# A three-product float32 matmul whose 512-column product is issued as two of 256 columns, in one block of a decoder trunk

## The chip, the cores and the metric

The kernel runs on one core of a Trainium2 chip. The metric is the device time of one execution in microseconds (us), lower is better. Engines are named as in the profile: PE is TensorE's matmul and PEld its weight load, DVE is VectorE, ACT is ScalarE, POOL is GpSimd, SP is the engine that issues most of the transfers.

## The reference, cut to what matters

Four residual layers over one stream of 256 tokens by 1024 features. Each layer is a token mixer and a squared-ReLU MLP, each behind an RMS norm. The second layer (index 1) has a block-sparse attention as its mixer, whose blocks are as long as the sequence, so that it is plain causal attention here.

```python
for i in range(DEPTH):                       # DEPTH = 4, mixers 0, 1, 2, 0
    a = rms_norm(h, attn_norm_g[i])
    ...
        y = moba_attention(a, moba_w_in[slot], moba_w_out[slot], cos, sin)
    ...
    h = h + y
    h = h + sqrelu_mlp(rms_norm(h, mlp_norm_g[i]), mlp_w_up[i], mlp_w_down[i])
```

`moba_attention` ends with `o @ w_out`, a product of 256x1024 with 1024x1024: the out projection. `sqrelu_mlp` is `(relu(h @ w_up) ** 2) @ w_down` with 4096 features between. All of it is float32.

## The kernel before, in words

**Numbers in two parts.** A float32 value is kept as a high part of type `float32r`, which TensorE multiplies at one pass, and a low part, the rest. A product is then three products: high by high, high by low and low by high. Weights come in 185 pieces of 128x2048 floats (1 MB each). `fetch` (L173) issues their transfers on SP. `stage` (L185) splits a piece in two halves of 1024 columns: ACT copies the high part (`whi`, L194), DVE subtracts it for the low part (`wlo`, L195). `take` (L204) hands out the next piece, with pieces staged two ahead (`LOOK`) and fetched five ahead (`FAR`). `whi` and `wlo` have three buffers each and `raw` four, so a piece is split only when TensorE has done with the piece three before it, and its transfer waits for the split of the piece four before it.

**A step.** Activations lie transposed, features on the partitions, as tiles of 128 x (2, 256): high parts of the 256 tokens, then low parts. `block_step` (L803) issues a step of one block of 128 outputs and one block of 128 inputs. One product takes the high weights with all 512 columns, into both halves of a PSUM bank; a second takes the low weights with the 256 high columns, into the bank's first half. Line L134 issues every matmul, so the profile tells them apart by their tiles alone. `joined` (L809) adds the halves: ACT copies the second (`cross`, L812), DVE adds (L813).

**The second layer's out projection** (`out_proj`, L848). Outputs 0 to 3 (128 features each) are accumulated in four banks `p_d`. Outputs 4 to 7 follow one after the other in banks `p_e`: for each of two weight pieces (`j`) and each of two blocks (`b`) eight steps over the inputs (`k`), whose activations are the tiles `oo`. After each block `into` (L815) adds the bank to the residual stream `hT` (DVE, L825), makes the normed stream's two parts `hg` (ACT L351, DVE L352) and its squares (ACT L356, DVE L361).

**The up projection** (`up_proj`, L866). Sixteen groups of two blocks, one piece of weights each, in banks `p_up` (four of them, so that a group reuses the banks of the group two before it). The first group goes over the inputs in the outer loop, so that it starts before the last `hg` is there, and the scheduler puts products of the second group between. Each group's banks are joined into `relu`, squared to `u` (DVE L890) and split to `uu` (ACT L892, DVE L893). In the second group's time the row of the norm is summed on POOL and its reciprocal taken on DVE (L1035). The down projection follows (`p_down`).

**What sets the order.** Each engine runs its instructions in the order of the program. A scheduler of the language makes that order from the dependencies, its own estimate of times and the pools' buffers; pairs listed by hand in `TURNS` set some orders of the mixers and the out projections, none of them in the block that the change touches.

Of the kernel before, what the change touches and what calls it, by code (L numbers as in the profile page):

```python
# [19 lines left out]
P = 128  # L20
# [131 lines left out]
def trunk(ctx: ExitStack, tc: tile.TileContext, xT, gains, lams, swa_row, fng, weights, out):  # L152
    nc = tc.nc
    V, A, G, T = nc.vector, nc.scalar, nc.gpsimd, Numbered(nc.tensor)
# [6 lines left out]
    def bank(tag, name):  # L161
        return ps.tile([P, 512], F32, tag=tag, name=name, bufs=4)
# [41 lines left out]
    def take():  # L204
        i = used[0]
        used[0] += 1
        while len(fetched) < min(weights.shape[0], i + FAR + 1):
            fetch()
        while len(staged) < min(weights.shape[0], i + LOOK + 1):
            stage()  # L210
        return staged[i]

    def r3(n):
        return lambda t: t.rearrange("p (a b) -> p a b", a=n)
# [586 lines left out]


    def block_step(p, hi, lo, x, start, stop, which="hl"):  # L803
        if "h" in which:
            T.matmul(r3(2)(p), hi, x, start=start, stop=False, skip_group_check=True)
        if "l" in which:
            T.matmul(p[:, :S], lo, x[:, 0], start=False, stop=stop, skip_group_check=True)
# [7 lines left out]
    def into(n, d, p, row, whole=False):  # L815

        j, b = d // 2, d % 2
        h = hT[j][:, S * b:S * b + S]
        y = p
        if not whole:  # L820
            y = sb.tile([P, S], F32, tag="y", name="y")
            joined(y, p)
        if row is not None:
            V.tensor_tensor(y, y, row, op=OP.mult)
        V.tensor_tensor(h, y, h, op=OP.add)  # L825
        norm_part(n, d)
        if b:
            norm_sum(n, j)
# [19 lines left out]
    def out_proj(parts, n, rest):  # L848

        banks = [bank("acc", f"p_d{j}") for j in range(4)]  # L850
        two = [[r3(4)(x) for x in take()] for _ in range(2)]
        order = [(k, d) for k in range(6) for d in range(4)] + [(k, d) for d in range(4) for k in (6, 7)]
        for k, d in order:
            hi, lo = (x[:, k % 4, P * d:P * d + P] for x in two[k // 4])
            block_step(banks[d], hi, lo, parts[k], k == 0, k == 7)
            if k == 7:
                into(n, d, banks[d], None)
        for j in range(2):
            hi, lo = (r3(8)(x) for x in take())
            for b in range(2):  # L860
                p = bank("acc", f"p_e{b}")
                for k in range(8):
                    block_step(p, hi[:, k, P * b:P * b + P], lo[:, k, P * b:P * b + P], parts[k], k == 0, k == 7)
                into(n, 4 + 2 * j + b, p, None)

    def up_proj(n, then):  # L866

        us = []
        for g in range(16):
            hi, lo = (r3(8)(x) for x in take())  # L870
            ps_up = [bank("wk", "p_up") for _ in range(2)]
            order = [(b, k) for b in range(2) for k in range(8)]
            if g == 0:
                order.sort(key=lambda x: x[1])

            def up(b, k, which):
                w = slice(P * b, P * b + P)
                block_step(ps_up[b], hi[:, k, w], lo[:, k, w], n.both[k // 2][:, k % 2], k == 0, k == 7, which)

            steps = [(x, "hl") for x in order]  # L880
            if g == 0:

                steps[7:10] = [(order[7 + x], w) for x, w in ((0, "h"), (1, "h"), (0, "l"), (2, "h"), (1, "l"), (2, "l"))]
            for (b, k), which in steps:
                up(b, k, which)
            t = sb.tile([P, 512], F32, tag="relu", name="relu")
            for b in range(2):
                joined(t[:, S * b:S * b + S], ps_up[b])
            u = sb.tile([P, 512], F32, tag="u", name="u")
            V.scalar_tensor_tensor(u, t, 0.0, t, op0=OP.max, op1=OP.mult)  # L890
            both = room(g, [P, 2, 2, S], "uu", F32R)
            A.activation(both[:, :, 0], r3(2)(u), AF.Copy)  # L892
            V.tensor_tensor(both[:, :, 1], r3(2)(u), f(both[:, :, 0]), op=OP.subtract)  # L893
            us += [both[:, b] for b in range(2)]
            then(g)
# [128 lines left out]
    for i in range(DEPTH):  # L1024
        T.layer = i
        parts, rest = mixer_layer(i, n)
# [98 lines left out]
```

## Time and profile before

| | us |
|---|---|
| three runs: lowest, median, highest | 1127.28, 1128.29, 1130.89 |
| the profiled execution | 1127.19 |
| its span, first to last instruction | 1125.4 |
| mean clock that TensorE was granted | 0.998 |

The costliest groups on TensorE, from the page: line, engine, operation, output and inputs, size, count, busy us and mean ns of one, idle time before them.

```profile
L134 PE MATMUL p_up<-hg,whi 128*128 128x512 f32 x1024 | 355.2, 394 | 0.0
L134 PE MATMUL p_up<-hg,wlo 128*128 128x256 f32 x1024 | 283.0, 277 | 0.0
L134 PE MATMUL p_down<-uu,whi 128*128 128x512 f32 x768 | 266.4, 394 | 0.0
```

The matmuls are pipelined: the durations of neighbours overlap, so that the mean of one is longer than the distance between two starts. Where a view gives the idle time before an instruction, what follows the arrow is the engine, tile and line that ended it. In a timeline, rows of one group that stand together are merged, with their count behind the x.

### The profile page before, as it was taken

The page shows a single profiled execution, that of the slowest core. Times are in us where ns is not written, and L with a number is a line of the kernel's source. Part 1 is how long each engine was busy: PE and PEld are TensorE (multiplying, and loading weights), DVE is VectorE, ACT ScalarE, POOL GpSimd, SP SyncE. Part 2 cuts the span into 40 slices and gives each one's busy share as a digit, 9 for nine tenths or more (in the row PEclk, how much of TensorE's full clock was granted, in tenths as well). Part 3 has the DMA queues.
Part 4 walks back from the last instruction along what each step waited for, and adds up shares of the span by engine and source line. Part 5 has one row for each costly group of instructions (what it writes and reads, how often), then busy time and mean ns, then how long its engine had stood idle before and what let it go on. Part 6 is the DMA issues. An engine that isn't in the chain of part 4 may idle for free.

```text
span 1125.4 us, 17122 instructions
## 1 busy us (share of the span) xinstructions
PE 1118.3 (99%) x6478; PEld 974.8 (87%) x6478; DVE 840.3 (75%) x1609; ACT 652.3 (58%) x1183; POOL 136.6 (12%) x273
## 2 busy tenths in 40 slices
PE   9999999999999999999999999999999999999997
PEld 7889888888888888888899998888888899888886
DVE  8888977656687798766569888765568788878453
ACT  7776666544476666554446765554446676555342
POOL 2250000000145200000000000000012410002800
PEclk9999999999999999999999999999999999999999
DMA  9533555555544446555563346555554444654551
GB/s 331 203 132 132 191 208 195 191 188 188 178 159 150 149 152 223 189 187 188 187 211 113 113 151 225 187 187 188 187 187 150 154 146 153 221 188 169 187 187 38
DMA packets 30466, 198.67 MB, mean 177 GB/s; under 512 B 3504, under 2 KB 5040, under 8 KB 7216
## 3 DMA queue, kind: packets, MB, share of 16 engines
q1 hardware_dynamic: 30096, 197.09, 50.6%
q8 instruction: 51, 0.84, 0.3%
q10 hardware_dynamic: 288, 0.49, 0.1%
q14 instruction: 31, 0.25, 0.1%
HBM read 196.52 MB, written 1.05 MB: 176 GB/s over the span
## 4 chain that ended last, share of the span: by engine, by line
PE 97%; DVE 1%; issue 1%; DMA 0%; SPq 0%; ACT 0%; POOLq 0%; POOL 0%; DVEq 0%
PE p_up L134 32%; PE p_down L134 24%; PE p_in L134 19%; PE p_last L134 7%; PE p_d L134 7%; PE p_s L134 3%; PE p_av L134 2%; PE p_qk L137 1%; PE p_t L137 1%; PE p_e L134 1%; DMA raw<-in_weights 0%; DVE wlo L195 0%; PE p_o L137 0%; DVE hg L352 0%; DVE acc L361 0%
## 5 line engine op out<-in xcount | busy, mean ns | idle before, releaser
L195 DVE TENSOR_TENSOR wlo<-raw,whi 128x1024 fp32r<-128x1024 f32 (+1 forms) x374 | 451.1, 1219 | 180.6 <-ACT whi L194 180.1
L194 ACT ACTIVATE whi<-raw 128x1024 fp32r<-128x1024 f32 (+1 forms) x374 | 383.8, 1045 | 200.3 <-issue 112.9
L134 PE MATMUL p_up<-hg,whi 128*128 128x512 f32 x1024 | 355.2, 394 | 0.0
L134 PE MATMUL p_up<-hg,wlo 128*128 128x256 f32 x1024 | 283.0, 277 | 0.0
L134 PE MATMUL p_down<-uu,whi 128*128 128x512 f32 x768 | 266.4, 394 | 0.0
L134 PEld LDWEIGHTS p_up<-hg,whi 128*128 128x128 f32 x1024 | 191.8, 188 | 44.0
L134 PE MATMUL p_down<-uu,wlo 128*128 128x256 f32 x768 | 212.7, 277 | 0.0
L134 PE MATMUL p_in<-whi,hg 128*128 128x512 f32 (+1 forms) x736 | 211.3, 370 | 0.0
L134 PEld LDWEIGHTS p_up<-hg,wlo 128*128 128x128 f32 x1024 | 192.3, 188 | 0.4
L134 PEld LDWEIGHTS p_down<-uu,whi 128*128 128x128 f32 x768 | 144.0, 188 | 33.4
L134 PEld LDWEIGHTS p_in<-whi,hg 128*128 128x128 f32 x736 | 132.3, 189 | 24.0 <-DVE hg L352 1.2
L134 PEld LDWEIGHTS p_down<-uu,wlo 128*128 128x128 f32 x768 | 144.2, 188 | 0.0
L134 PE MATMUL p_in<-wlo,hg 128*128 128x512 f32 (+1 forms) x368 | 130.1, 368 | 0.1
L892 ACT ACTIVATE uu<-u 128x512 fp32r<-128x512 f32 x64 | 40.4, 632 | 80.2 <-DVE u L890 80.2
L134 PE MATMUL p_d<-oo,whi 128*128 128x256 f32 (+1 forms) x416 | 85.2, 296 | 0.0
L134 PE MATMUL p_last<-whi,uu 128*128 128x512 f32 (+1 forms) x264 | 79.4, 383 | 0.0
L134 PEld LDWEIGHTS p_in<-wlo,hg 128*128 128x128 f32 x368 | 68.8, 189 | 11.5 <-DVE wlo L195 0.5
L812 ACT ACTIVATE cross<-p_up 128x256 f32<-128x256 f32 x128 | 47.9, 374 | 35.5 <-PE p_up L134 34.1
L134 PEld LDWEIGHTS p_d<-oo,whi 128*128 128x128 f32 x416 | 66.3, 191 | 1.9 <-issue 0.2
L351 ACT ACTIVATE hg<-hT,gn 128x256 fp32r<-128x256 f32 x64 | 31.4, 503 | 60.5 <-DVE hT L825 60.5
L476 ACT ACTIVATE e<-ns,nm 128x128 f32<-128x128 f32 (+1 forms) x128 | 56.8, 446 | 13.8 <-DVE nm L473 13.8
L518 POOL MEMSET kpadh<- 64x512 f32 x8 | 4.2, 521 | 494.3 <-PE p_down L134 494.1
(179 smaller groups left out, 1235.1 us busy)
## 6 DMA issues: line engine op xcount, KB each, us to landing
raw<-in_weights SPq DMA_DIRECT2D x181, 1024.0 KB, 4.9
raw<-in_weights SPq DMA_DIRECT2D x8, 256.0 KB, 4.8
raw<-in_weights SPq DMA_DIRECT2D x4, 512.0 KB, 7.0
hT<-in_xT SPq DMA_DIRECT2D x8, 128.0 KB, 4.7
bias<-in_swa_row SPq DMA_DIRECT2D x1, 512.0 KB, 4.2
grow<-in_fng SPq DMA_DIRECT2D x1, 512.0 KB, 3.8
lv<-in_lams SPq DMA_DIRECT2D x1, 256.0 KB, 6.6
out<-given ACTq DMA_DIRECT2D x1, 256.0 KB, 2.7
```

What stands on the lines that cost most here:

```text
L134: return self.keep(out.tensor.name.rstrip("_0123456789"), self.engine.matmul(out, *args, **kw))
L137: return self.keep(out.tensor.name.rstrip("_0123456789"), self.engine.transpose(out, *args, **kw))
L194: high = A.activation(hi[:, s], raw[:, s], AF.Copy)
L195: low = V.tensor_tensor(lo[:, s], raw[:, s], f(hi[:, s]), op=OP.subtract)
L351: A.activation(both[:, 0], h, AF.Copy, scale=g)
L476: A.activation(e[:, s], ns[:, s], AF.Exp, bias=nm[:, t:t + 1], scale=-1.0, accum_out=l[:, t:t + 1])
L518: G.memset(f(kpad[x][HD * (1 - h):HD * (1 - h) + HD, :, h, :]), 0.0)
L812: A.activation(cross, p[:, S:], AF.Copy)
L892: A.activation(both[:, :, 0], r3(2)(u), AF.Copy)
```

## The change

In the last block of the second layer's out projection (`j` = 1, `b` = 1, outputs 896 to 1023) the product of the high weights with 512 columns is issued as two products of 256 columns: with the activations' high parts into the bank's first half, then with their low parts into its second half. The product with the low weights stays. This is done for each of the eight `k`. Only the first product of the block starts the bank. The arithmetic is the same.

```diff
     def block_step(p, hi, lo, x, start, stop, which="hl"):
+        if "H" in which:
+
+            for h in range(2):
+                T.matmul(r3(2)(p)[:, h], hi, x[:, h], start=start and h == 0, stop=False, skip_group_check=True)
         if "h" in which:
             T.matmul(r3(2)(p), hi, x, start=start, stop=False, skip_group_check=True)
         if "l" in which:
...
                 for k in range(8):
-                    block_step(p, hi[:, k, P * b:P * b + P], lo[:, k, P * b:P * b + P], parts[k], k == 0, k == 7)
+                    block_step(p, hi[:, k, P * b:P * b + P], lo[:, k, P * b:P * b + P], parts[k], k == 0, k == 7,
+                               "Hl" if j and b else "hl")
                 into(n, 4 + 2 * j + b, p, None)
```

The orders of the two built programs, compared engine by engine (buffer numbers aside): TensorE has 6362 products instead of 6354, eight of 512 columns being sixteen of 256. Besides, one product moves: ahead of the first group's last four products (those with the last tile `hg3`'s second block) stood five products of the second group, now four, and the fifth follows behind the four.

```text
before: p_up (group 2) x5, p_up (group 1)<-hg3 x4, p_up (group 2) ...
after:  p_up (group 2) x4, p_up (group 1)<-hg3 x4, p_up (group 2) ...
```

In the following two groups ACT and DVE take a few instructions in another order (the splits of pieces 68 and 69 against `cross`, `relu`, `u` and `uu` of the second and third groups), and SP's transfer of piece 73 waits for one more semaphore. From the fourth group on, and ahead of the changed block, the orders are the same.

## The prediction

> **What bounds the kernel now.** I read the page first: its busy line, its slices of the granted clock, and the shares of the chain that ended last.
>
> ```profile
> span 1125.4 us, 17122 instructions
> PE 1118.3 (99%) x6478; PEld 974.8 (87%) x6478; DVE 840.3 (75%) x1609; ACT 652.3 (58%) x1183; POOL 136.6 (12%) x273
> ...
> PEclk9999999999999999999999999999999999999999
> ...
> PE 97%; DVE 1%; issue 1%; DMA 0%; SPq 0%; ACT 0%; POOLq 0%; POOL 0%; DVEq 0%
> ```
>
> TensorE is busy 99% of the span, and 97% of the chain is its matmuls. The kernel is a stream of products at an undiminished clock, so a change on TensorE counts in full unless a wait lies behind it, and a change elsewhere counts only if TensorE comes to stand. Next I read the chain of waits in order of time, at the place of the change:
>
> ```profile
> 386.50 5.88 PE p_d L134 x33
> 392.37 11.09 PE p_e L134 x64
> 403.47 88.83 PE p_up L134 x512
> 492.30 88.75 PE p_down L134 x512
> ```
>
> The 64 products of `p_e` give the features 512 to 1023 of the second layer's out projection. The last 16 of them are changed (8 with the high weights, 8 with the low). The up projection follows with no gap. Its 512 products and those of the down projection have the same shapes, 256 pairs of 512 and 256 columns, yet take 88.83 and 88.75 us: some 0.08 us are lost in the up projection. That loss becomes a term below.
>
> **The products themselves.** The timeline of TensorE shows the pace. The columns are start, duration, engine, line, operation; durations overlap, so the pace is the distance of the starts.
>
> ```profile
> 400.53 0.39 PE L134 MATMUL p_e<-oo,whi 128*128 128x512 f32 x1
> ...
> 402.96 0.39 PE L134 MATMUL p_e<-oo,whi 128*128 128x512 f32 x1
> 403.19 0.28 PE L134 MATMUL p_e<-oo,wlo 128*128 128x256 f32 x1
> ```
>
> These are the first and the last high product of the changed block. Seven steps in 402.96 - 400.53 = 2.43 us are 0.347 us for a step of 512 + 256 columns, and the 512 take 403.19 - 402.96 = 0.23 of them. After the change a step is three products of 256 columns, the first two with the same weights. The trace has just that pattern, in the third layer's out projection: high weights twice, low weights once, each of 256 columns.
>
> ```profile
> 644.22 0.28 PE L134 MATMUL p_d<-oo,wlo 128*128 128x256 f32 x1
> ...
> 651.42 0.28 PE L134 MATMUL p_d<-oo,wlo 128*128 128x256 f32 x1
> ```
>
> Twenty steps lie between these two rows, so a step takes 7.20 / 20 = 0.360 us. The change removes 8 products of 512 columns and adds 16 of 256 with 8 more weight loads; it costs 8 x (0.360 - 0.347) = **0.10 us**, directly on the path. The bounds: if a product of 256 columns takes half of one of 512, 8 x (2 x 0.115 - 0.23) = 0; if every added weight load were exposed, what the rival below gives. I take 0.10, from the row with the same shapes, weights and order. A window over that stretch shows why the halves do not get cheaper, and that the clock holds:
>
> ```profile
> 644.20:651.40 7.20, 7.20 (x62) 7.20 (x61) 0.38 (x1) 0.00 (x0) 1.00 0.33 108
> ```
>
> TensorE's weight loads (the fourth column) fill 7.20 of 7.20 us there at clock 1.00: with 256 columns the loads stand back to back, and the pace is theirs. The Trainium skill, "TensorE: Matmul & The Clock Gate", section "Back-to-back issue gap", gives the isolated gap as the columns over 2.4 plus 2.5 ns; two halves would cost 2.5 ns more than the whole, by which I estimate 0.02 us for the eight steps. The trace disagrees in size (0.10), not in sign, and the measurement stands.
>
> **What the instruction order adds.** I compared the two built programs engine by engine. Besides the split there is one move on TensorE. The up projection's first group must end with the last block of the normed stream (`hg3`), which is made from the changed block. While that is made, TensorE has products of the second group as fillers: five before, four after. The fifth (512 columns, `hg1` with the second group's weights) moves behind the four products that need `hg3`. Whether that costs depends on whether TensorE waits there now. It does, a little:
>
> ```profile
> 408.51 0.48 DVE L352 SCALAR_TENSOR_TENSOR hg<-hT,gn,hg 128x256 fp32r<-128x256 f32 x1 [0.58 <-ACT hg L351]
> ...
> 405.73 0.63 PE L134 MATMUL p_up<-hg,whi 128*128 128x512 f32 x2
> ...
> 408.86 0.69 PE L134 MATMUL p_up<-hg,whi 128*128 128x512 f32 x2
> 409.39 0.28 PE L134 MATMUL p_up<-hg,wlo 128*128 128x256 f32 x1
> ...
> 408.75 0.49 PEld L134 LDWEIGHTS p_up<-hg,whi 128*128 128x128 f32 x2
> ```
>
> VectorE finishes the low part of `hg3` at 408.51 + 0.48 = 408.99. The last filler starts at 408.86. Two products of 512 columns in a row take 0.63 us when nothing waits (the row at 405.73) and 0.69 here: the second starts at 408.86 + 0.69 - 0.39 = 409.16 instead of 409.09. Its weight load, which carries the wait, starts at 408.75 + 0.49 - 0.19 = 409.05, just after 408.99. So 0.07 us of waiting, the loss seen above, and at this place the end is set by the chain that makes `hg3`, not by TensorE's own work. With one filler fewer TensorE arrives at 409.09 + 0.10 - 0.23 = 408.96 and waits until `hg3` is there. It has the filler of **0.23 us** still to do afterwards. The cover of that filler is gone, and it counts whole.
>
> Is `hg3` itself later? I followed it back:
>
> ```profile
> 403.38 1.06 ACT L194 ACTIVATE whi<-raw 128x1024 fp32r<-128x1024 f32 x1 [1.05 <-PE p_e L134]
> 404.18 0.43 DVE L825 TENSOR_TENSOR hT<-y,hT 128x256 f32<-128x256 f32 x1
> 404.52 1.22 DVE L195 TENSOR_TENSOR wlo<-raw,whi 128x1024 fp32r<-128x1024 f32 x1
> 405.65 0.48 DVE L352 SCALAR_TENSOR_TENSOR hg<-hT,gn,hg 128x256 fp32r<-128x256 f32 x1
> 406.05 0.42 DVE L813 TENSOR_TENSOR y<-p_e,cross 128x256 f32<-128x256 f32 x1
> 406.38 1.21 DVE L195 TENSOR_TENSOR wlo<-raw,whi 128x1024 fp32r<-128x1024 f32 x1
> 407.52 0.42 DVE L825 TENSOR_TENSOR hT<-y,hT 128x256 f32<-128x256 f32 x1
> 407.97 0.51 ACT L351 ACTIVATE hg<-hT,gn 128x256 fp32r<-128x256 f32 x1 [1.87 <-DVE hT L825]
> ...
> 431.21 1.06 ACT L194 ACTIVATE whi<-raw 128x1024 fp32r<-128x1024 f32 x1
> 432.30 1.23 DVE L195 TENSOR_TENSOR wlo<-raw,whi 128x1024 fp32r<-128x1024 f32 x1 [0.29 <-ACT whi L194]
> ```
>
> VectorE goes without a break from 404.18 to 407.94; the sum with the changed bank (406.05) starts long after that bank is full at 403.47, so the end of the block is not on the chain. What is on it: ScalarE splits the next weights at 403.38, as soon as the last high product (402.96 + 0.39 = 403.35) lets their buffer go. Their low part follows on VectorE at 404.52, though `whi` ended at 403.38 + 1.06 = 404.44. Where VectorE waits for ScalarE alone, it starts 0.03 after (the last two rows: 431.21 + 1.06 = 432.27, then 432.30). After the change the second half of the last high product ends at 400.53 + 7 x 0.360 + 0.12 + 0.28 = 403.45. So `whi` ends 0.10 later, 404.54, and `wlo` starts at about 404.57, **0.05 us** later; everything behind it moves as much. The bounds are 0 (VectorE stays bound by its own order) and 0.10; I take the middle, 0.05.
>
> **The other moves.** In the groups behind, VectorE takes the low part of the weights of piece 68 earlier, ScalarE splits piece 69 after the second bank of the third group instead of before it, and VectorE takes 69's low part behind one `u` and one `uu` more. What hides this is the lead on TensorE:
>
> ```profile
> 414.57 1.06 ACT L194 ACTIVATE whi<-raw 128x1024 fp32r<-128x1024 f32 x1 [1.98 <-PE p_up L134]
> ...
> 423.86 1.21 DVE L195 TENSOR_TENSOR wlo<-raw,whi 128x1024 fp32r<-128x1024 f32 x1
> 425.00 0.68 DVE L890 SCALAR_TENSOR_TENSOR u<-relu 128x512 f32<-128x512 f32 x1
> 425.60 0.42 DVE L813 TENSOR_TENSOR relu<-p_up,cross 128x256 f32<-128x256 f32 x1
> 426.38 0.69 DVE L893 TENSOR_TENSOR uu<-u,uu 128x512 fp32r<-128x512 f32 x1 [0.36 <-ACT uu L892]
> ...
> raw<-in_weights SPq DMA_DIRECT2D x181, 1024.0 KB, 4.9
> ```
>
> A group takes 88.83 / 16 = 5.55 us; the sixth, which uses piece 69, starts at 403.47 + 5 x 5.55 = 431.2. Piece 69 is ready at 423.86 + 1.21 = 425.07 now, and after 0.68 + 0.69 + about 0.4 of waiting at about 426.9. That leaves 4.3 us: nothing on the path, 0 to the sum. SP's transfer of piece 73 gets a further wait, for that later split; behind it in SP's queue stand all later transfers. It lands 4.9 us after its issue, by about 432, and is split only when the seventh group has let its buffer go, at 403.47 + 7 x 5.55 = 442.3. So this costs nothing either. From the fourth group on the orders are the same.
>
> **Sum.** The 0.10 us of the split are not added to the rest: TensorE waits for `hg3` behind them, so they vanish in that wait. The end moves by the delay of `hg3` and the uncovered filler: 0.05 + 0.23 = **0.28 us**. The profiled execution took 1127.19 us (span 1125.4), the median of the three runs is 1128.29. On the median this gives 1128.57, so **1128.6 us**, +0.02%. A measurement of this kernel can tell about 0.3% (3.4 us) from no change; this is a twelfth of it.
>
> **Rivals.**
> *The filler is not missed* (9%). If the wait at `hg3` is an accident of that one execution, the moved product costs nothing and only the split stays: +0.10, 1128.4. For it: the wait is only 0.07 us. Against it: TensorE waits already, and after the change it arrives 0.13 us earlier than now.
>
> *The added weight loads are exposed* (7%). The tile view of `p_e` has their price.
>
> ```profile
> L134 PEld LDWEIGHTS p_e<-oo,whi x32: 187/187/187, 392.1 to 402.8; 128*128 128x128 f32 x32
> ```
>
> Eight loads of 0.187 us that stood between the products would add 1.5 us; `hg3` would come later by about as much, so 0.23 + 1.5 on the median, 1130.0. For it: the loads fill all of the window at 644 to 651. Against it: the same pattern at 644 to 651 runs at 0.120 us a product, less than one load, so loads overlap. The Trainium skill's page "TensorE: Matmul & The Clock Gate", section "What overlaps and what doesn't" (under the measured mechanism of tiles), says that a load overlaps running products only where the row group differs; by that rule this rival would be the result. The trace speaks against the rule for these full-height loads: 0.120 us from start to start with loads of 0.187.
>
> *Slower: VectorE's new order holds up a bank* (4%). The second bank of the second group is now read behind `wlo` of piece 68, and the second bank of the fourth group, which reuses it, starts at 403.47 + 3 x 5.55 + 2.77 = 422.9. That `wlo` waits for `whi` of piece 68, whose first half ends at 414.57 + 1.06 = 415.63. With `wlo` (1.21), `uu` (0.69) and the bank's sum (0.42) between, TensorE stands once that half ends after 422.9 - 2.3 = 420.6, 5.0 us later than now. A transfer that missed its turn (4.9 us of landing and a group of 5.55) would pass this by 5.5 us: 1128.3 + 0.3 + 5.5 = 1134.1. Against it: ScalarE waited there for TensorE (1.98 us), not for a transfer.
>
> *Faster* has no mechanism of its own: nothing on the path gets shorter. Only the spread of the medians could show it.
>
> **How the numbers follow.** The forecast has 80%; the rivals 9, 7 and 4. The first two lie within 0.3% too. Slower by over 0.3% holds the 4% of the bank and 1% for the spread of medians, faster 2% for that spread, the rest, 93%, is within. The range takes the three runs (1127.28 to 1130.89) moved by 0.28 and the two small rivals, from **1127.2 to 1131.2 us**. It leaves out the held bank.
>
> **What would show it.** In the changed kernel's trace: steps of three at 0.36 us in the last `p_e` block; ScalarE's split of the next weights about 0.1 us later after the block's start; TensorE's wait ahead of `hg3` grown from 0.07 to about 0.25 us, four fillers ahead of it; 512 products of the up projection in about 89.0 us, measured from the end of `p_e`, instead of 88.83; no other stand of TensorE in that layer, and the same distances behind it. I am wrong if `p_e` takes over 11.3 us (now 11.09), if TensorE stands at a `whi` or a bank between 410 and 435, or if the time moves by over 3.4 us, which none of these rows could make.

## The result and the profile after

| | before | changed |
|---|---|---|
| median of 22 runs, us | 1127.66 | 1131.11 |
| lowest to highest | 1126.78 to 1131.71 | 1127.02 to 1131.96 |
| runs above 1129.5 | 2 of 22 | 18 of 22 |
| profiled execution (span) | 1127.19 (1125.4) | 1131.47 (1129.7) |

The ratio is 1.0021, 95% interval 1.0013 to 1.0028: slower, and less than the 0.3% that was set as the bound. The time lies in the predicted range. But the number cannot be read without one fact that the prediction missed: the runs of both kernels fall into two clusters, at about 1127.5 and 1131, with none between 1129.1 and 1130.8. The change moves runs from the lower to the upper one.

The chain of waits of the changed kernel, in order of time, at the place where the prediction read it (start, duration, engine, tile, line, count):

```profile
392.88 11.36 PE p_e L134 x72
404.24 90.62 PE p_up L134 x512
494.86 90.46 PE p_down L134 x512
```

These are 11.36, 90.62 and 90.46 us, where before had 11.09, 88.83 and 88.75. The whole difference of the spans, 4.3 us, is in four pieces: 0.5 ahead of `p_e` (392.88 against 392.37), 0.27 in `p_e`, 1.79 in the up projection and **1.71 in the down projection**, which the change does not touch and whose products are the same in the same order. Behind it nothing more is lost. The 0.5 are not the change's: most of them stand already at the first layer's up projection (118.77 against 118.39 in the two chains), where the orders are the same. The down projection's 256 pairs take 90.46 / 256 = 353.4 ns each instead of 88.75 / 256 = 346.7. No wait explains that: here is a stretch of the timeline of TensorE in the changed kernel,

```profile
450.18 0.40 PE L134 MATMUL p_up<-hg,whi 128*128 128x512 f32 x1
...
453.36 0.40 PE L134 MATMUL p_up<-hg,whi 128*128 128x512 f32 x1
```

and the same in the kernel before:

```profile
450.19 0.40 PE L134 MATMUL p_up<-hg,whi 128*128 128x512 f32 x1
...
453.31 0.39 PE L134 MATMUL p_up<-hg,whi 128*128 128x512 f32 x1
```

Nine pairs take 3.18 us in the one and 3.12 in the other, evenly, each product following the one before. A window over the down projection of the changed kernel gives the granted clock:

```profile
500.00:580.00 80.00, 80.00 (x455) 69.37 (x454) 46.02 (x59) 35.54 (x46) 0.00 (x0) 1.00 0.54 186
```

It is 1.00, as before. TensorE has **two paces** for an alternation of 512 and 256 columns, and they last. The timeline shows where they change in the changed kernel's profile:

```profile
398.02 0.40 PE L134 MATMUL p_e<-oo,whi 128*128 128x512 f32 x1
...
401.20 0.40 PE L134 MATMUL p_e<-oo,whi 128*128 128x256 f32 x2
...
407.61 0.40 PE L134 MATMUL p_up<-hg,whi 128*128 128x512 f32 x1
...
409.35 0.39 PE L134 MATMUL p_up<-hg,whi 128*128 128x512 f32 x1
...
409.80 0.50 PE L134 MATMUL p_up<-hg,whi 128*128 128x512 f32 x1
...
410.26 0.39 PE L134 MATMUL p_up<-hg,whi 128*128 128x512 f32 x1
...
413.79 0.40 PE L134 MATMUL p_up<-hg,whi 128*128 128x512 f32 x1
```

Ahead of the split nine pairs take 401.20 - 398.02 = 3.18 us: the slower pace, already there (24 such pairs at 6.7 ns are 0.16 of the 0.27 us in `p_e`). Behind the split it goes on, up to the first group's swap (two high products in a row, at 406.55). Ahead of the wait for `hg3`, five pairs take 409.35 - 407.61 = 1.74, 348 ns each: the faster one. The row at 409.80 is the product that waits. Behind it ten pairs take 413.79 - 410.26 = 3.53: the slower pace, which then lasts to the end of the down projection. The price is 512 pairs x 6.7 ns = 3.4 us for the two projections, the distance between the clusters.

### The profile page after: what moved, and what is told of

Read it like the earlier page. It is cut to its first block, busy times and chain, and to the rows that moved or that the text cites. A ratio compares the mean times of both kernels' runs of the same rounds, so it can differ in the third digit from the quotient of the medians.

```text
span 1129.7 us, 17137 instructions
## 1 busy us (share of the span) xinstructions
PE 1121.8 (99%) x6486; PEld 976.6 (86%) x6486; DVE 840.6 (74%) x1609; ACT 652.2 (58%) x1183; POOL 136.5 (12%) x273
## 4 chain that ended last, share of the span: by engine, by line
PE 97%; DMA 1%; issue 0%; SPq 0%; DVE 0%; ACT 0%; POOLq 0%; POOL 0%; DVEq 0%
PE p_up L134 32%; PE p_down L134 24%; PE p_in L134 19%; PE p_last L134 7%; PE p_d L134 7%; PE p_s L134 3%; PE p_av L134 2%; PE p_qk L137 1%; PE p_t L137 1%; DMA raw<-in_weights 1%; PE p_e L134 1%; PE p_o L137 0%; SPq L227 0%; SPq L180 0%; DVE wlo L195 0%
```

## The experiments

The theory after the result: **the pace is a state of TensorE's stream that lasts while the alternation goes on, and the filler that was taken away made the wait for `hg3` longer, out of which TensorE comes in the slower pace.** Rivals: the split products themselves bring the slower pace; or the new orders of VectorE and ScalarE slow the groups. All experiments touch the second layer alone. The table sums them up; "upper" counts runs above 1129.5 us. Ratios are to the kernel before on the same chip.

| kernel | median us | lowest to highest | upper | ratio (95%) |
|---|---|---|---|---|
| `e1_split_five` | 1127.80 | 1126.95 to 1131.52 | 4 of 12 | 1.0003 (0.9991 to 1.0014) |
| `e2_whole_four` | 1130.98 | 1130.38 to 1131.72 | 12 of 12 | 1.0020 (1.0010 to 1.0031) |
| `e3_split_reset` | 1127.67 | 1127.19 to 1128.70 | 0 of 12 | 0.9992 (0.9982 to 1.0002) |
| `e4_split_seven` | 1130.43 | 1127.44 to 1131.56 | 8 of 12 | 1.0014 (1.0002 to 1.0026) |
| `e5_whole_reset` | 1128.91 | 1127.37 to 1131.09 | 6 of 12 | 1.0007 (0.9995 to 1.0018) |
| `e6_whole_two` | 1129.63 | 1127.72 to 1131.24 | 6 of 12 | 1.0010 (0.9998 to 1.0022) |
| `e7_split_six` | 1130.62 | 1127.27 to 1131.15 | 6 of 10 | 1.0014 (1.0001 to 1.0026) |
| `e8_split_seven_again` | 1131.01 | one run | 1 of 1 | |
| `e9_whole_double` | 1128.26 | 1127.65 to 1129.42 | 0 of 12 | 0.9990 (0.9978 to 1.0002) |
| `e10_whole_even` | 1129.45 | 1126.89 to 1131.60 | 6 of 12 | 1.0002 (0.9987 to 1.0017) |
| `e11_whole_group` | 1127.40 | 1126.98 to 1130.85 | 3 of 12 | 0.9992 (0.9979 to 1.0006) |
| `e12_split_group` | 1130.46 | 1127.31 to 1132.34 | 8 of 12 | 1.0013 (1.0000 to 1.0026) |

The kernel before, run beside them on four chips, had 12 of 35, 7 of 29, 10 of 23 and 9 of 23 in the upper cluster, about a third, so its 2 of 22 above are few; whether by luck or by the chip is not known. (One more of the 29 is a lone run of 1379 us.)

**The split alone, the order of before (`e1_split_five`).** Two pairs are added to the list of the second layer's turns: the first block's product with `hg3` behind the fifth filler, and the second block's behind the first's. TensorE's order is then that of the kernel before, with the split in it.

```diff
         (("p_s", 18), ("p_in", 144)),
+        (("p_up", 28), ("p_up", 36)),
+        (("p_up", 30), ("p_up", 29)),
```

> The change with TensorE's order of the kernel before: five fillers ahead of the last normed block, the split kept, VectorE's and ScalarE's orders in the second and third groups about those of the changed kernel. Theory wait (the pace of the up and down projections of the second layer, 0.347 or 0.353 us a pair, is set by how TensorE comes out of its wait for hg3, and the filler taken away made that wait longer): the time falls back to most runs near 1127.7, median 1127.5 to 1128.5, up projection near 88.9 us. Theory split (the split products bring TensorE into the slow pace by themselves): stays near 1131.1, up projection near 90.6 us. Theory order (the new orders of VectorE and ScalarE slow the groups): stays near 1131.1 too.

Median 1127.80, 4 of 12 upper, like the kernel before. Its chain:

```profile
392.02 11.19 PE p_e L136 x72
403.21 88.82 PE p_up L136 x512
492.03 88.75 PE p_down L136 x512
```

`p_e` takes 11.19 us, 0.10 more than 11.09, with the faster pace ahead of the split: the predicted cost of the split, to the hundredth. The up projection takes 88.82 where it took 88.83. So the split products do not bring the lasting slower pace; nor do the orders of VectorE and ScalarE, which here, read tile by tile up to the down projection, are those of the changed kernel. For a short stretch the pairs behind the split do run slower:

```profile
403.05 0.40 PE L136 MATMUL p_up<-hg,whi 128*128 128x512 f32 x1
...
405.52 0.64 PE L136 MATMUL p_up<-hg,whi 128*128 128x512 f32 x2
...
406.58 0.40 PE L136 MATMUL p_up<-hg,whi 128*128 128x512 f32 x1
...
408.66 0.63 PE L136 MATMUL p_up<-hg,whi 128*128 128x512 f32 x2
```

Seven pairs take 405.52 - 403.05 = 2.47 us, 353 ns each, though the pace ahead of the split was the faster one. Behind the first group's swap at 405.52 six pairs take 408.66 - 406.58 = 2.08, 347 each. In all seven profiles with the split the pairs directly behind it have the slower pace; in five of them the first group's swap ends it, in two (`e4_split_seven`, `e12_split_group`) it does not.

**The order of the changed kernel, no split (`e2_whole_four`).**

```diff
         (("p_s", 18), ("p_in", 144)),
+        (("p_up", 36), ("p_up", 31)),
+        (("p_up", 48), ("p_up", 31)),
```

> The kernel before, 512 columns whole, with the order of the changed kernel on TensorE: four fillers ahead of the last normed block. Theory wait: most runs near 1131, median 1130 to 1131.3, up projection near 90.6 us. Theory split: as before, median 1127.5 to 1128.2, plus at most 0.3. Theory order: near 1131, since VectorE's order is near that of the changed kernel.

All 12 runs are upper. The weight load that carries the wait stands 0.34 us for `hg3`, and the projections behind it have the slower pace (the chain has the first 32 products of the up projection apart):

```profile
409.66 0.19 PEld L136 LDWEIGHTS p_up<-hg,whi 128*128 128x128 f32 x1 [0.34 <-DVE hg L354]
```

```profile
404.08 5.56 PE p_up L136 x32
409.66 85.06 PE p_up L136 x480
494.71 90.46 PE p_down L136 x512
```

One product's place, with no product added, is enough for the whole loss. With `e1_split_five`, where the split and the new orders of VectorE and ScalarE stand without the loss, this settles which part of the change does it.

**A swap in the third group (`e3_split_reset`).** The changed kernel, where the third group begins with two high products and then their two low ones, once:

```diff
+            if T.layer == 1 and g in RESET:
+
+                steps[0:2] = [(order[x], w) for x, w in ((0, "h"), (1, "h"), (0, "l"), (1, "l"))]
             for (b, k), which in steps:
```

> The changed kernel with one swap in the third group of the second layer's up projection: two products with the high weights, then the two with the low ones, once, a pattern after which the changed kernel's trace goes from the slow pace to the fast one (at 406.7). Theory wait, with a pace that lasts until something disturbs it: slow up to the third group, fast after it, so 1131.1 less some 480 pairs of 6.7 ns, 3.2 us: median 1127.5 to 1128.5. Theory order, and a slow pace that belongs to the stage and not to a state of TensorE: 1131.1.

No run of 12 is upper; median 1127.67. The timeline shows the pair of high products, and the chain the down projection back at 88.75:

```profile
414.96 0.64 PE L135 MATMUL p_up<-hg,whi 128*128 128x512 f32 x2
415.44 0.40 PE L135 MATMUL p_up<-hg,wlo 128*128 128x256 f32 x2
```

```profile
403.65 89.14 PE p_up L135 x512
492.79 88.75 PE p_down L135 x512
```

Four products in another order, some 10 us behind the change, take back nearly all of the loss. That the slower pace is a lasting state, which a broken alternation can end, is shown by this.

**No wait at all (`e4_split_seven`).** The changed kernel with seven fillers ahead of `hg3`.

```diff
         (("p_s", 18), ("p_in", 144)),
+        (("p_up", 28), ("p_up", 38)),
+        (("p_up", 30), ("p_up", 29)),
```

> The changed kernel with seven fillers ahead of the last normed block, so that TensorE does not wait for it at all. Theory wait: no wait, and the fast pace of the products before it goes on; nearly all runs near 1127.5, and fewer slow runs than the kernel before has, median 1127.2 to 1127.9. Theory split: 1131.

A miss: 8 of 12 runs are upper. So the wait is not the only thing that sets the pace. The profiled run was a lower one, without a wait at `hg3`.

**The swap without the change (`e5_whole_reset`).** The edit of `e3_split_reset` on the kernel before.

> The kernel before, nothing split, with the one swap in the third group (two high products, then their two low ones). Theory reset (that pattern brings TensorE into the fast pace from either pace): no run near 1131, where the kernel before has about one in three there; median about 1127.4, highest below 1129, ratio of means about 0.999. Theory toggle (the pattern only disturbs, and the pace after it is drawn anew): slow runs remain, one in three or more.

6 of 12 are upper: the swap does not bring the faster pace from everywhere. In the profiled run it did the reverse. Its alternation was in the faster pace up to the swap, and the projections behind it have the slower one:

```profile
414.79 0.62 PE L135 MATMUL p_up<-hg,whi 128*128 128x512 f32 x2
415.24 0.40 PE L135 MATMUL p_up<-hg,wlo 128*128 128x256 f32 x2
```

```profile
403.76 90.33 PE p_up L135 x512
494.08 90.45 PE p_down L135 x512
```

The expectation's theory of a reset falls. Its rival, that the pace is drawn anew, is borne out in that upper runs remain; but a draw that forgets what came before would give `e3_split_reset` and this kernel the same share, and they had 0 and 6 of 12. In the two profiled runs the swap exchanged the paces: slower to faster there, faster to slower here. An exchange would turn the 18 of 22 upper runs of the changed kernel into about 2 of 12, and the third of the kernel before into about 8 of 12. The counts allow that, but no experiment tests it by itself.

**A longer wait (`e6_whole_two`).** The kernel before with two fillers.

```diff
         (("p_s", 18), ("p_in", 144)),
+        (("p_up", 34), ("p_up", 31)),
+        (("p_up", 48), ("p_up", 31)),
```

> The kernel before, nothing split, with two fillers ahead of hg3 instead of five, so that TensorE's wait there grows by 0.35 us over that with four. Theory length (a long wait leaves the slow pace): all runs slow, 1131.0 to 1131.9. Theory phase (the pace after a wait depends on the instant at which TensorE goes on, not on the length): another share of slow runs than with four fillers (12 of 12), down to none, then about 1127.9 to 1128.5 with the longer wait.

TensorE stands twice as long, and yet only 6 of 12 are upper. The profiled run comes to its wait of 0.69 us in the faster pace and leaves it in the faster pace:

```profile
409.28 0.19 PEld L136 LDWEIGHTS p_up<-hg,whi 128*128 128x128 f32 x1 [0.69 <-DVE hg L354]
```

```profile
409.28 83.82 PE p_up L136 x482
493.10 88.75 PE p_down L136 x512
```

So it is not "the longer the wait, the slower"; the length alone does not decide.

**Another broken place (`e7_split_six`).** As `e3_split_reset`, with six products in the order of the first group's own swap.

```diff
-                steps[0:2] = [(order[x], w) for x, w in ((0, "h"), (1, "h"), (0, "l"), (1, "l"))]
+                steps[0:3] = [(order[x], w) for x, w in ((0, "h"), (1, "h"), (0, "l"), (2, "h"), (1, "l"), (2, "l"))]
```

> The changed kernel with the other swap, that of the first group (high, high, low, high, low, low), put into the third group instead of the four-product one. Theory reset by any two high products in a row: as with the four-product swap, 1127.2 to 1128.5 in every run. If only the four-product pattern does it: 1131, or a mixture.

A mixture, 6 of 10 upper. Two high products in a row do not suffice for a reset, and an exchange of the paces at each such place, which would make about 2 of 10 out of 18 of 22, does not give 6 of 10 either.

**Where a run without a wait turns (`e8_split_seven_again`).** The kernel of `e4_split_seven` once more, to catch an upper run.

> Another look at the kernel with seven fillers, to find where its slow runs become slow (8 of 12 were near 1131, its profiled run was not). If this run is slow: theory wait says that a wait of over 0.05 us stands ahead of the slow stretch in the up projection; theory state says that the slow pace comes from ahead of the first group or from its swap, without a wait.

This one is upper. It can be laid beside the lower run of the same program. At the odd filler's place (two high products in a row, then high, low, low) the run at 1131.01 has

```profile
409.81 0.62 PE L136 MATMUL p_up<-hg,whi 128*128 128x512 f32 x2
410.26 0.28 PE L136 MATMUL p_up<-hg,wlo 128*128 128x256 f32 x1
```

and the run at 1127.93

```profile
409.97 0.64 PE L136 MATMUL p_up<-hg,whi 128*128 128x512 f32 x2
410.45 0.28 PE L136 MATMUL p_up<-hg,wlo 128*128 128x256 f32 x1
```

Neither waits there. The pace turned from the faster to the slower one in the first and the other way in the second: the same instructions, and the projections behind take 90.45 and 88.75 us. In all rows of this kind shown here (0.64 at `e3_split_reset` and here: faster behind; 0.62 at `e5_whole_reset` and here: slower behind) the distance of the two tells what follows. The first group's swap fits it: its two high products take 0.64 in the five profiles with the split where the pace is faster behind, and 0.62 in `e4_split_seven` and `e12_split_group`, where it stays slower. That is an association, not a cause.

**Another regular pattern (`e9_whole_double`).** The kernel before with high, high, low, low throughout, from the second group of the up projection to the end of the down projection.

```diff
+            if T.layer in DOUBLE and g:
+
+                steps = [(x, w) for j in range(0, 16, 2) for w in "hl" for x in order[j:j + 2]]
             for (b, k), which in steps:
...
-                for k in range(16):
-                    block_step(p, hi[:, k], lo[:, k], us[16 * h + k], h + k == 0, h == 1 and k == 15)
+                steps = [(k, "hl") for k in range(16)]
+                if T.layer in DOUBLE:
+                    steps = [(k, w) for j in range(0, 16, 2) for w in "hl" for k in (j, j + 1)]
+                for k, which in steps:
+                    block_step(p, hi[:, k], lo[:, k], us[16 * h + k], h + k == 0, h == 1 and k == 15, which)
```

> The kernel before, nothing split, with the second layer's up projection (from its second group) and down projection in pairs of steps throughout: high, high, low, low instead of high, low. Theory state (alternating 512 and 256 columns have two lasting paces, 346.7 and 353.3 ns for two products, and which one holds is settled where the alternation is broken): another pattern has a pace of its own, the same in every run, so the spread of 3.5 us between runs shrinks; at 346.7 the median is near 1127.4, at 353.3 near 1131. Rival (the slow runs come from something outside TensorE's order, such as the transfers): the two clusters of runs stay, 1127.5 and 1131.

One cluster: 1127.65 to 1129.42, while the kernel before on the same chip had 10 of 23 runs upper.

```profile
403.53 89.24 PE p_up L135 x512
492.77 89.17 PE p_down L135 x512
```

89.17 / 256 = 348.3 ns for two products, between the two paces and near the better one. The same arithmetic, products and weights give one cluster of times in this order and two in the other, on one chip, so the clusters need the order on TensorE; transfers or the chip's condition do not make them alone. Only one run of this order was profiled: that the others had its pace is read from their times.

**No broken place (`e10_whole_even`).** The kernel before without the first group's swap, and with eight fillers, so that 512 and 256 columns alternate from the out projection to the end of the down projection.

```diff
-            if g == 0:
+            if g == 0 and T.layer != 1:
...
         (("p_s", 18), ("p_in", 144)),
+        (("p_up", 28), ("p_up", 39)),
+        (("p_up", 30), ("p_up", 29)),
```

> The kernel before, nothing split, with the alternation unbroken from the out projection to the end of the down projection: no swap in the first group, eight fillers, so no two products of the same kind in a row, and TensorE does not wait for hg3. Theory state: the profiled run has one pace from its last out projection blocks to the end of the down projection, 346.7 or 353.3, whichever it came with; runs in two clusters, 1127.4 and 1131, the share of each that of the state ahead (in ten profiles the out projection was fast seven times). Rival (each stage or each group settles its pace by itself): the pace changes within the stretch.

```profile
392.46 11.09 PE p_e L136 x64
403.55 88.75 PE p_up L136 x512
492.30 88.75 PE p_down L136 x512
```

The profiled run keeps one pace throughout, 88.75 twice, and loses nothing at `hg3`. Half of the runs are upper all the same. None of these was profiled, so their pace ahead is not shown. The nearest reading is that, with nothing to turn it, the pace is that with which TensorE comes out of the mixer; that this differs from run to run is shown by the other profiles, where the pairs of `p_e` ahead of the changed block had the slower pace in 4 of 14.

**A doubled group (`e11_whole_group`, `e12_split_group`).** The third group alone in the pattern high, high, low, low, on the kernel before and on the changed one.

```diff
+            if (T.layer, g) == DOUBLE:
+
+                steps = [(x, w) for j in range(0, 16, 2) for w in "hl" for x in order[j:j + 2]]
             for (b, k), which in steps:
```

> The kernel before, nothing split, with only the third group of the second layer's up projection in pairs of steps (high, high, low, low, sixteen times), and high, low from the fourth group on. Theory state, if the doubled pattern forgets the pace that it came with: after it the alternation starts from one state, so all runs fall into one cluster, 1127.2 to 1128.0 if it is the fast pace, 1131 if it is the slow one, and the kernel with the split and the same third group falls into the same cluster. If the doubled pattern keeps a memory: two clusters as with one swap (6 of 12 slow).

> The changed kernel with the same third group (high, high, low, low, sixteen times). If the doubled pattern forgets: the same single cluster as the kernel without the split, 0.1 to 0.4 us above it. If it keeps a memory: another share of slow runs than without the split, as one swap gave (none of 12 here against 6 of 12 there).

3 of 12 and 8 of 12: two clusters in both. In the profiled runs the pace behind the doubled group is the one ahead of it, slower in the first and faster in the second. The doubled pattern does not make TensorE forget how it came, so this is no way to force the faster pace.

The profile of `e12_split_group` shows one thing more. Its wait for `hg3`, with four fillers as in the changed kernel, led the other way:

```profile
408.00 0.40 PE L135 MATMUL p_up<-hg,whi 128*128 128x512 f32 x1
...
409.76 0.40 PE L135 MATMUL p_up<-hg,whi 128*128 128x512 f32 x1
...
410.21 0.19 PEld L135 LDWEIGHTS p_up<-hg,whi 128*128 128x128 f32 x1 [0.25 <-DVE hg L353]
...
411.01 0.39 PE L135 MATMUL p_up<-hg,whi 128*128 128x512 f32 x1
...
412.74 0.40 PE L135 MATMUL p_up<-hg,whi 128*128 128x512 f32 x1
```

Five pairs ahead of the wait take 409.76 - 408.00 = 1.76 us, 352 ns each; five behind it take 412.74 - 411.01 = 1.73, 346 each. So a wait of this length does not lead into the slower pace as such. In all five profiles with four fillers (this one, the changed kernel, `e2_whole_four`, `e3_split_reset`, `e7_split_six`; waits of 0.25 to 0.34 us) the pace behind the wait is the other one than ahead of it: four times faster to slower, once slower to faster.

**What all fourteen profiles agree on.** The pace of the second layer's down projection goes with the run's time. It takes 90.45 or 90.46 us in the five upper runs, 88.75 in eight of the lower ones and 89.17 in `e9_whole_double`. The down projections of the first and the third layer take 88.75 in every one.

**What stays open.** What in the chip makes two paces is not visible in any of these traces. That the wait with four fillers exchanges the paces, and ends in the slower one so often (18 of 22 with the split, 12 of 12 without) because TensorE mostly comes to it in the faster one, fits the five profiles, of which only one came in the slower pace; no run forces it. Why the longer wait with two fillers leaves half of the runs upper is not settled: the instant at which TensorE goes on, against its own rhythm, is a guess that these runs allow but do not show.

The quickest version with the split is `e3_split_reset`: 1127.67 against 1131.11 for the changed kernel, and 0.9992 (0.9982 to 1.0002) of the kernel before. Its gain over the kernel before is not clear of no change, and it lies in the missing upper runs.

## Why the prediction was right or wrong, point by point

- *The split costs 0.10 us.* Right: 11.19 against 11.09 in `e1_split_five`, to which some 0.05 us come in the seven slower pairs behind it (7 x 6.7 ns). In the changed kernel's profile the eight steps take 404.08 - 401.20 = 2.88 us, 0.360 each, as read off the third layer. The row at 401.20 stands above; the next stage starts at 404.08:

```profile
404.08 0.40 PE L134 MATMUL p_up<-hg,whi 128*128 128x512 f32 x1
```

That the weight loads set this pace ("the pace is theirs") was argued from loads that fill the window, and no run here tests it: loads of 187 ns that start 120 apart fill any window and overlap one another.

- *TensorE's wait ahead of `hg3` grows to about 0.25 us, behind four fillers.* Right, it is 0.26:

```profile
409.80 0.19 PEld L134 LDWEIGHTS p_up<-hg,whi 128*128 128x128 f32 x1 [0.26 <-DVE hg L352]
```

- *ScalarE's split is 0.10 us later, `hg3` 0.05.* The first is right (404.16, 2.96 us behind the block's start, against 2.85), and VectorE's low part now waits for it, as predicted. `hg3` is 0.09 later: 409.26 + 0.49 lies 8.55 behind the block's start, against 8.46. That is within the bounds of 0 and 0.10, and not their middle.

```profile
404.16 1.06 ACT L194 ACTIVATE whi<-raw 128x1024 fp32r<-128x1024 f32 x1 [1.34 <-PE p_e L134]
405.25 1.23 DVE L195 TENSOR_TENSOR wlo<-raw,whi 128x1024 fp32r<-128x1024 f32 x1 [0.18 <-ACT whi L194]
409.26 0.49 DVE L352 SCALAR_TENSOR_TENSOR hg<-hT,gn,hg 128x256 fp32r<-128x256 f32 x1 [0.58 <-ACT hg L351]
```

- *The other moves cost nothing.* Right: `e1_split_five` has the same orders on VectorE and ScalarE, and its up projection takes 88.82.
- *The up projection in about 89.0 us, and the same distances behind it.* **Wrong, and this is the step that failed**: 90.62, and 90.46 for a down projection that was not touched. "Seven steps in 2.43 us are 0.347 us for a step" was taken as the price of a step everywhere, when it is one of two, and the stages behind the first group were put at no loss at all, without asking what their pace hangs on. What the runs showed instead is that the moved filler changes the pace: 353.4 ns a pair for some 500 pairs. The sentence that no row could make 3.4 us was false by that: an unremarkable 6.7 ns, times 512 pairs, is 3.4 us.
- *Wrong if `p_e` takes over 11.3 us, or if the time moves by over 3.4.* By these signs of its own the prediction was wrong: `p_e` takes 11.36, and the medians lie 3.45 apart. The first is not the split but the slower pace of the 24 pairs ahead of it; `e1_split_five`, with the faster pace there, has 11.19.
- *Within 0.3%, with 93%, and between 1127.2 and 1131.2 us.* Right, but by less than it looks, by luck, and not by the sum. The range holds 1131.11 only because its upper end is the run at 1130.89, itself an upper run. The sum was 0.28 us, and apart from the pace the traces give about that: 0.10 for the split, and 0.19 for the wait that grew from 0.07 to 0.26. What was measured, 1.0021 or 2.4 us, is what the share of runs that moved makes, (18 - 2) / 22 of 3.4 us, 2.5 us, and the 0.28 cannot be seen in it. Against the later runs of the kernel before, 38 of 110 upper, the same 18 of 22 would be a move of (0.82 - 0.35) x 3.4 = 1.6 us.
- *The rivals.* The added loads were not exposed, no bank was held up, and the moved filler was missed. The rival that was needed, a wait that leaves TensorE in another pace, was not among them. The times of before had it in plain sight: three runs at 1127.28, 1128.29 and 1130.89, which the prediction took for spread.

## What to carry to other kernels

Where a kernel is one stream of matmuls, look at the runs' times one by one before you price a small edit: two clusters can mean a state that lasts, and an edit that costs 0.1 us can move runs by the distance between them. Then compare a stage that the edit does not touch, by its time over its count: 90.46 against 88.75 for the same 512 products showed at once that the loss was not one wait. Where single runs matter, an order with one pace can be worth more than the one with the best pace: high, high, low, low cost 1.6 ns a pair more than the better pace here and held all runs within 1.8 us.

## What the runs showed of the hardware that was not expected

- TensorE ran an unbroken alternation of `float32r` products with 512 and 256 columns, each with its own weights, at 346.7 or at 353.4 ns a pair, at a granted clock of 1.00 in both, over some 500 pairs without a change (`e10_whole_even`, the changed kernel).
- In the profiled runs the pace changed only where the alternation was broken (products of the same size in a row) or where TensorE waited. Waits of 0.25 to 0.34 us led four times from the faster into the slower pace and once the other way; 0.69 us left the faster pace as it was. The same program gave either pace in different runs (`e4_split_seven` and `e8_split_seven_again`).
- Products of 512, 512, 256, 256 columns ran at 348.3 ns for a product of each size in the profiled run of `e9_whole_double`; its 12 times lie within 1.8 us.
- Three products of 256 columns, two with the same weights, took 360 ns, 120 each, while each weight load took 187 to 192: loads overlapped products and one another.
